# A 128-token unit of a gated recurrence: scores relative to the end of its first 64-token chunk, so that one pair of operands serves scores, output and state update

## The chip, the cores and the metric

The kernel runs on one core of a Trainium2 chip (trn2). The metric is the device time of one execution in microseconds; the kernel before took 1212.33 us, the median of three runs (1212.31 to 1212.84).

## What is computed

One inference step of a layer with three gated branches: 1024 prompt tokens and 32 sample tokens of width 1024 are normalised, multiplied with one combined weight matrix of 8192 columns, sent through branches A, B and C, merged and projected. The change lies in branch A alone, a gated linear recurrence with 4 heads of 128 columns, in chunks of 64 tokens:

```python
def step(s, inp):
    qc, lc, kc, vc = inp
    b = jnp.cumsum(lc, axis=2)
    qg = qc * jnp.exp(b)
    kg = kc * jnp.exp(-b)
    att = jnp.where(mask, jnp.einsum('bhtk,bhsk->bhts', qg, kg), 0.0)
    o = jnp.einsum('bhts,bhsv->bhtv', att, vc) + jnp.einsum('bhtk,bhkv->bhtv', qg, s)
    b_last = b[:, :, -1:, :]
    s = jnp.exp(b_last[:, :, 0, :])[..., None] * s + jnp.einsum('bhsk,bhsv->bhkv', kc * jnp.exp(b_last - b), vc)
    return s, o
```

Here `b` is the running sum of the log gates within a chunk, `qg` and `kg` are the query and key with the decay put in, and `s` is the state (128x128 per head). Afterwards each head's output is normalised, gated and projected down. The final states of prompt and sample are outputs too.

## The kernel before

Tokens stand in three groups of 384, 384 and 288 columns (the last holds 256 prompt and 32 sample tokens). All dense products are three-term: an operand is split into a high and a low part in a reduced float format, and each product is issued as high by high, high by low, low by high, so that one slot (`slot`) of 8 blocks is 24 matmuls at line 60 (`issue`). Weights come in tiles of 128 columns; `wprep` splits the next tile on ScalarE (`whi`, line 40) and VectorE (`wlo`, line 43) while the present one is used.

The order on each engine is that of the program (a manual schedule). The side work is written as generators that each slot advances: those in the list `fast` one step in the middle of a slot of 24 matmuls and one at its end, those in `slow` one step per slot. So a step of branch A's recurrence stands between stretches of 12 dense matmuls.

Branch A works head by head (`branch_a(j)`). Its four weight tiles give the forget gate, value, query and output gate (`psfa`, `psva`, `psqa`, `psga`). `chain` (in `slow`) makes the log gates, their running sum `b` by a scan that restarts every 64 tokens, `eb = exp(b)`, `kg = exp(-b)` times the key (lines 742, 743, 761) and `kd`, the key with the decay to its chunk's end (lines 746, 755, 762). `ev_va` and `tr_va` bring the values out of PSUM and transpose them on TensorE (lines 698, 706).

`hgrn` (in `fast`) then walks over 9 units: 8 of 128 prompt tokens, which are two chunks each, and one of 32 sample tokens. Its stages are staggered: step `t` issues `u0(t)`, `u2(t-1)`, `u4(t-2)`, `u3(t-1)`, `u1(t)`.

- `prep(g)` (lines 788 to 793, GpSimd) makes a second pair of operands for a group: `kd2`, the keys decayed to the end of the whole unit, and `qg2`, the queries with the decay from the unit's start.
- `u0` on TensorE: the scores within the chunks (line 807, `kg` by `qg`, 128x128), the scores of the second chunk's queries with the first chunk's keys (line 810, 64 columns of `kd` by 64 of `qg`, into 64x64), and a transpose of `kd2` (line 812).
- `u1`: VectorE puts the masked scores into `attm` (line 817) and the 64x64 block beside them (line 819); ScalarE copies the transposed keys out as `kt` (line 821).
- `u2` on TensorE: the state's increment (line 828, `kt` by `v`), the output from the scores (line 829), and the output from the old state `S` (line 831, with `qg2`).
- `u3`: VectorE makes the new state (line 842, old state times decay plus increment), ScalarE the square sum `sq` for the norm (line 849), GpSimd its inverse root (lines 155, 156).
- `u4` and `fin`: the scaled output `on` (line 856), three transposes back (line 863) and the gate (line 865).

The sample unit has no line 810. So a head issues line 810 eight times.

Of the kernel before, what the change touches and what calls it, by code (L numbers as in the profile page):

```python
# [7 lines left out]
F32 = mybir.dt.float32  # L8
# [3 lines left out]
OP = mybir.AluOpType  # L12
# [15 lines left out]
def kernel(ctx: ExitStack, tc: tile.TileContext, I, O):  # L28
# [647 lines left out]
    nc.gpsimd.memset(bd[0:64, 64:128], 0.0)  # L676
# [9 lines left out]
    def branch_a(j):  # L686
        R = {}
        f, lf, b, eb, kg, kd, va, qg, sg, el = {}, {}, {}, {}, {}, {}, {}, {}, {}, {}
        vs = ap.tile([32, 128], F32, tag="vs", name="vs")
        S0 = ap.tile([128, 128], F32, tag="S0", bufs=1, name="S0")  # L690

        def c64(t, g):
            nf = 6 if g < 2 else 4
            return t[:, :nf * 64].rearrange("p (c t) -> p c t", t=64), nf
# [29 lines left out]
        def chain():  # L724
            nc.sync.dma_start(S0, I["state_hgrn"][0, 0, j])
            for g in range(3):
                f[g] = T(g, "f")
                nc.scalar.activation(f[g], R["psfa", g], AF.Sigmoid)
                nc.vector.tensor_scalar(f[g], f[g], oml[:, j:j + 1], lb[:, j:j + 1], op0=OP.mult, op1=OP.add)
                if g < 2:  # L730
                    yield
# [8 lines left out]
            for g in range(3):  # L740
                eb[g], kg[g] = T(g, "eb"), T(g, "kg")
                nc.scalar.activation(eb[g], b[g], AF.Exp)
                nc.scalar.activation(kg[g], b[g], AF.Exp, scale=-1.0)
                bv, nf = c64(b[g], g)
                lv, _ = c64(lf[g], g)
                nc.vector.tensor_tensor(lv, bv[:, :, 63:64].to_broadcast([128, nf, 64]), bv, op=OP.subtract)
                if g == 2:
                    nc.vector.tensor_scalar(lf[g][:, 256:288], b[g][:, 256:288], -1.0, b[g][:, 287:288],
                                            op0=OP.mult, op1=OP.add)
# [3 lines left out]
            for g in range(3):  # L753
                kd[g] = lf[g]
                nc.scalar.activation(kd[g], lf[g], AF.Exp)
                ev, nf = c64(eb[g], g)
                el[g] = small.tile([128, 8], F32, tag="el", bufs=6, name="el")
                nc.gpsimd.tensor_copy(el[g][:, :nf], ev[:, :, 63])
                if g == 2:
                    nc.gpsimd.tensor_copy(el[g][:, 4:5], eb[g][:, 287:288])  # L760
                nc.vector.tensor_tensor(kg[g], kg[g], f[g], op=OP.mult)
                nc.gpsimd.tensor_tensor(kd[g], kd[g], f[g], op=OP.mult)
# [15 lines left out]
        def hgrn():  # L778
            qg2, kd2, elp, on = {}, {}, {}, {}

            def prep(g):
                npair = 3 if g < 2 else 2
                w = npair * 128
                qg2[g], kd2[g] = T(g, "qg2"), T(g, "kd2")
                v4 = lambda t: t[:, :w].rearrange("p (c h t) -> p c h t", h=2, t=64)
                eh = el[g][:, :2 * npair].rearrange("p (c h) -> p c h", h=2)
                bc = lambda h: eh[:, :, h:h + 1].to_broadcast([128, npair, 64])
                nc.gpsimd.tensor_scalar(v4(kd2[g])[:, :, 1, :], v4(kd[g])[:, :, 1, :], 1.0, 0.0, op0=OP.mult, op1=OP.add)
                nc.gpsimd.tensor_tensor(v4(kd2[g])[:, :, 0, :], v4(kd[g])[:, :, 0, :], bc(1), op=OP.mult)
                nc.gpsimd.tensor_scalar(v4(qg2[g])[:, :, 0, :], v4(qg[g])[:, :, 0, :], 1.0, 0.0, op0=OP.mult, op1=OP.add)  # L790
                nc.gpsimd.tensor_tensor(v4(qg2[g])[:, :, 1, :], v4(qg[g])[:, :, 1, :], bc(0), op=OP.mult)
                elp[g] = small.tile([128, 4], F32, tag="elp", name="elp")
                nc.gpsimd.tensor_tensor(elp[g][:, :npair], eh[:, :, 0], eh[:, :, 1], op=OP.mult)

            units = [(g, c) for g in range(3) for c in range(3)]
            nu = len(units)
            pu, po, at, kt, rs, Ss = {}, {}, {}, {}, {}, {-1: None}
# [6 lines left out]
            def u0(u):  # L804
# [3 lines left out]
                if not smp:  # L808
                    c0 = c * 128
                    nc.tensor.matmul(p[0:64, 128:192], kd[g][:, c0:c0 + 64], qg[g][:, c0 + 64:c0 + 128],  # L810
                                     start=True, stop=True)
                nc.tensor.transpose(p[:m, 192:320], kd[g][:, sl] if smp else kd2[g][:, sl], ident)  # L812

            def u1(u):
# [3 lines left out]
                if not smp:  # L818
                    nc.vector.tensor_copy(a[0:64, 64:128], pu[u][0:64, 128:192])
                kt[u] = ap.tile([128, 128], F32, tag="kt", name="kt")  # L820
                nc.scalar.activation(kt[u][:m], pu[u][:m, 192:320], AF.Copy)

            def u2(u):
                g, c, smp, m, sl = geo(u)
                vv = vs if smp else va[g][:, sl]
                S = S0 if smp else Ss[u - 1]
                po[u] = abank("po")
                nc.tensor.matmul(pu[u][:, 320:448], kt[u][:m], vv, start=True, stop=True)
                nc.tensor.matmul(po[u][:m, 0:128], at[u][:m, :m], vv, start=True, stop=(S is None))
                if S is not None:  # L830
                    nc.tensor.matmul(po[u][:m, 0:128], qg[g][:, sl] if smp else qg2[g][:, sl], S,
                                     start=False, stop=True)

            def u3(u):
                g, c, smp, m, sl = geo(u)
                S = S0 if smp else Ss[u - 1]
                Sn = Ss[u] = ap.tile([128, 128], F32, tag="S", bufs=3, name="S")
# [303 lines left out]
```

## Time and profile before

| | |
|---|---|
| runs | 1212.31, 1212.33, 1212.84 us |
| profiled execution, first to last instruction (its span) | 1210.8 us |
| TensorE (PE) busy | 1193.9 us, 99% |
| PE's weight loads (PEld), which overlap it | 1170.2 us, 97% |
| VectorE (DVE) busy | 548.6 us, 45% |
| ScalarE (ACT) busy | 477.0 us, 39% |
| GpSimd (POOL) busy | 267.5 us, 22% |
| mean granted TensorE clock | 0.998 of full |

For the profiled execution the span is the time that is shown; the runs' median is 1.5 us longer. Busy time of PE is a model: matmuls are pipelined, each lasts longer than the distance to the next one's start, and so the price of a matmul is read as the distance between two starts in the timeline, not as its duration. A plain fp32 matmul is one line of the program and two on PE (x2 in the timeline); a transpose and a split product are one.

### The profile page before, as it was taken

The page shows a single profiled execution, that of the slowest core. Times are in us where ns is not written, and L with a number is a line of the kernel's source. Part 1 is how long each engine was busy: PE and PEld are TensorE (multiplying, and loading weights), DVE is VectorE, ACT ScalarE, POOL GpSimd, SP SyncE. Part 2 cuts the span into 40 slices and gives each one's busy share as a digit, 9 for nine tenths or more (in the row PEclk, how much of TensorE's full clock was granted, in tenths as well). Part 3 has the DMA queues.
Part 4 walks back from the last instruction along what each step waited for, and adds up shares of the span by engine and source line. Part 5 has one row for each costly group of instructions (what it writes and reads, how often), then busy time and mean ns, then how long its engine had stood idle before and what let it go on. Part 6 is the DMA issues. An engine that isn't in the chain of part 4 may idle for free.

```text
span 1210.8 us, 18948 instructions
## 1 busy us (share of the span) xinstructions
PE 1193.9 (99%) x7630; PEld 1170.2 (97%) x7630; DVE 548.6 (45%) x1088; ACT 477.0 (39%) x1015; POOL 267.5 (22%) x478
## 2 busy tenths in 40 slices
PE   7999999999999999999999999999999999999998
PEld 7899999999999999999999999999999999999996
DVE  4957775257611234454545421223465541337322
ACT  6567667366711114252525221111344452224211
POOL 3413222022201242333323201223000001224101
PEclk9999999999999999999999999999999999999999
DMA  8521101211111121010111111102111112105321
GB/s 263 172 64 38 40 21 44 79 37 38 44 42 39 44 62 53 19 51 27 45 33 43 35 48 35 53 27 75 44 45 38 29 45 70 54 27 174 105 92 40
DMA packets 113564, 70.65 MB, mean 58 GB/s; under 512 B 5560, under 2 KB 109668, under 8 KB 113476
## 3 DMA queue, kind: packets, MB, share of 16 engines
q1 hardware_dynamic: 113476, 69.44, 19.1%
q8 instruction: 60, 0.98, 0.3%
q14 instruction: 28, 0.23, 0.1%
HBM read 63.49 MB, written 5.93 MB: 57 GB/s over the span
## 4 chain that ended last, share of the span: by engine, by line
PE 94%; DVE 2%; DMA 2%; ACT 1%; issue 1%; SPq 0%; POOL 0%; POOLq 0%; DVEq 0%; ACTq 0%
PE psz L60 23%; PE psdn L60 15%; PE psout L60 8%; PE psgb L60 8%; PE psxb L60 7%; PE psfa L60 4%; PE psva L60 4%; PE psga L60 4%; PE psqc L60 4%; PE psqa L60 4%; PE psgc L60 3%; PE pr L60 1%; PE pi L60 1%; PE poc L60 1%; PE pu L812 1%; PE pssa L60 1%
## 5 line engine op out<-in xcount | busy, mean ns | idle before, releaser
L43 DVE TENSOR_TENSOR wlo<-wraw,whi 128x1024 fp32r<-128x1024 f32 (+1 forms) x100 | 107.9, 1079 | 263.1 <-ACT whi L40 261.9
L60 PE MATMUL psz<-hh,whi 128*128 128x384 f32 (+1 forms) x576 | 185.9, 323 | 0.0
L60 PE MATMUL psz<-hh,wlo 128*128 128x384 f32 (+1 forms) x576 | 185.1, 321 | 0.0
L60 PE MATMUL psz<-hl,whi 128*128 128x384 f32 (+1 forms) x576 | 185.0, 321 | 0.0
L40 ACT ACTIVATE whi<-wraw 128x1024 fp32r<-128x1024 f32 (+1 forms) x104 | 96.3, 926 | 82.9 <-PE psdn L60 74.1
L60 PE MATMUL psdn<-pl,whi 128*128 128x384 f32 (+1 forms) x384 | 124.2, 323 | 0.0
L60 PE MATMUL psdn<-ph,whi 128*128 128x384 f32 (+1 forms) x384 | 124.1, 323 | 0.0
L60 PE MATMUL psdn<-ph,wlo 128*128 128x384 f32 (+1 forms) x384 | 124.1, 323 | 0.0
L60 PEld LDWEIGHTS psz<-hh,whi 128*128 128x128 f32 x576 | 108.1, 188 | 0.7 <-issue 0.6
L60 PEld LDWEIGHTS psz<-hh,wlo 128*128 128x128 f32 x576 | 108.2, 188 | 0.3 <-DVE wlo L43 0.3
L60 PEld LDWEIGHTS psz<-hl,whi 128*128 128x128 f32 x576 | 108.1, 188 | 0.0
L584 ACT ACTIVATE sz<-psz 128x384 f32<-128x384 f32 (+1 forms) x72 | 33.3, 463 | 181.8 <-PE psz L60 181.7
L60 PEld LDWEIGHTS psdn<-ph,whi 128*128 128x128 f32 x384 | 72.1, 188 | 0.0
L60 PEld LDWEIGHTS psdn<-pl,whi 128*128 128x128 f32 x384 | 72.1, 188 | 0.0
L60 PEld LDWEIGHTS psdn<-ph,wlo 128*128 128x128 f32 x384 | 72.1, 188 | 0.0
L60 PE MATMUL psout<-hh,mhi 128*128 128x384 f32 (+3 forms) x216 | 68.8, 319 | 0.0
L60 PE MATMUL psout<-hh,mlo 128*128 128x384 f32 (+3 forms) x216 | 68.8, 319 | 0.0
L60 PE MATMUL psout<-hl,mhi 128*128 128x384 f32 (+3 forms) x216 | 68.8, 318 | 0.0
L60 PE MATMUL psxb<-hh,wlo 128*128 128x384 f32 (+1 forms) x192 | 62.1, 324 | 0.0
L60 PE MATMUL psxb<-hh,whi 128*128 128x384 f32 (+1 forms) x192 | 61.9, 323 | 0.0
L60 PE MATMUL psxb<-hl,whi 128*128 128x384 f32 (+1 forms) x192 | 61.8, 322 | 0.0
L60 PE MATMUL psgb<-hh,whi 128*128 128x384 f32 (+1 forms) x192 | 61.8, 322 | 0.0
(308 smaller groups left out, 2957.9 us busy)
## 6 DMA issues: line engine op xcount, KB each, us to landing
wraw<-in_w_in SPq DMA_DIRECT2D x64, 512.0 KB, 4.1
xt<-in_x_prompt SPq DMA_DIRECT2D x8, 512.0 KB, 5.2
wraw<-in_w_b_down SPq DMA_DIRECT2D x16, 256.0 KB, 2.8
wraw<-in_w_out SPq DMA_DIRECT2D x8, 512.0 KB, 3.8
xf<-in_x_prompt SPq DMA_DIRECT2D x8, 512.0 KB
out<-yf SPq DMA_DIRECT2D x8, 512.0 KB, 2.9
wraw<-in_w_mem_k SPq DMA_DIRECT2D x4, 512.0 KB, 4.1
wraw<-in_w_mem_v SPq DMA_DIRECT2D x4, 512.0 KB
```

The costliest lines, as they stand in the source:

```text
L40: nc.scalar.activation(out, in_, AF.Copy)
L43: (eng or nc.vector).tensor_tensor(out, a, hi.bitcast(F32), op=OP.subtract)
L60: nc.tensor.matmul(ps, a, b, start=st, stop=sp)
L584: nc.scalar.activation(s, R["psz", g], AF.Sigmoid)
L812: nc.tensor.transpose(p[:m, 192:320], kd[g][:, sl] if smp else kd2[g][:, sl], ident)
```

## The change

Within a unit the running sums are shifted so that both chunks count from the end of the first chunk. For the first chunk VectorE subtracts the sum at its last token (`dm`, taken out by small GpSimd copies) from `b` before the two exponentials. Then `kg` and `qg` give all scores of the unit in one 128x128 product under a plain triangular mask, the transposed `kg` serves the state update, and `qg` serves the output from the state. What is carried from unit to unit is now `R`, the state relative to that point (VectorE); ScalarE makes `Sn` from it with one factor per row, `dec`, which stands in `qg`'s frame and is what the next unit's matmul reads. `prep`, `kd`, `kd2`, `qg2`, `el`, `elp`, line 810's matmul and line 819's copy go.

```diff
--- before.py
+++ after.py
@@ -667,13 +667,12 @@
     down(lambda k: prods_b[4 + k], C_ZB, "second", AH_B)
     ap = next_phase("ap", 2)
     bd = ap.tile([128, 128], F32, bufs=1, name="bd")
     nc.gpsimd.memset(bd, 1.0)
     nc.gpsimd.affine_select(bd, bd, pattern=[[1, 128]], compare_op=OP.is_ge, fill=0.0,
                             base=0, channel_multiplier=-1)
-    nc.gpsimd.memset(bd[0:64, 64:128], 0.0)
     attm = [ap.tile([128, 128], F32, bufs=1, name=f"attm{i}") for i in range(2)]
     for t in attm:
         nc.gpsimd.memset(t, 0.0)
@@ -685,13 +684,11 @@
     def branch_a(j):
         R = {}
-        f, lf, b, eb, kg, kd, va, qg, sg, el = {}, {}, {}, {}, {}, {}, {}, {}, {}, {}
+        f, lf, b, eb, kg, va, qg, sg = {}, {}, {}, {}, {}, {}, {}, {}
         vs = ap.tile([32, 128], F32, tag="vs", name="vs")
         S0 = ap.tile([128, 128], F32, tag="S0", bufs=1, name="S0")
-
-        def c64(t, g):
-            nf = 6 if g < 2 else 4
-            return t[:, :nf * 64].rearrange("p (c t) -> p c t", t=64), nf
+        dm = ap.tile([128, 20], F32, tag="dm", name="dm")
+        dec = ap.tile([128, 9], F32, tag="dec", name="dec")
         def ev_va(g):
             vT = T(g, "vT")
@@ -723,6 +720,7 @@
         def chain():
             nc.sync.dma_start(S0, I["state_hgrn"][0, 0, j])
+            nc.gpsimd.memset(dm[:, 8:10], 0.0)
             for g in range(3):
                 f[g] = T(g, "f")
                 nc.scalar.activation(f[g], R["psfa", g], AF.Sigmoid)
@@ -738,28 +736,26 @@
             ev_va(0)
             yield
             for g in range(3):
+                npair = 3 if g < 2 else 2
                 eb[g], kg[g] = T(g, "eb"), T(g, "kg")
+                bv = b[g][:, :npair * 128].rearrange("p (c h t) -> p c h t", h=2, t=64)
+                u = 3 * g
+                nc.gpsimd.tensor_copy(dm[:, u:u + npair], bv[:, :, 0, 63])
+                nc.gpsimd.tensor_copy(dm[:, 10 + u:10 + u + npair], bv[:, :, 1, 63])
+                nc.vector.tensor_tensor(bv[:, :, 0, :], bv[:, :, 0, :],
+                                        dm[:, u:u + npair].unsqueeze(2).to_broadcast([128, npair, 64]),
+                                        op=OP.subtract)
+                if g == 2:
+                    nc.gpsimd.tensor_copy(dm[:, 18:19], b[g][:, 287:288])
                 nc.scalar.activation(eb[g], b[g], AF.Exp)
                 nc.scalar.activation(kg[g], b[g], AF.Exp, scale=-1.0)
-                bv, nf = c64(b[g], g)
-                lv, _ = c64(lf[g], g)
-                nc.vector.tensor_tensor(lv, bv[:, :, 63:64].to_broadcast([128, nf, 64]), bv, op=OP.subtract)
-                if g == 2:
-                    nc.vector.tensor_scalar(lf[g][:, 256:288], b[g][:, 256:288], -1.0, b[g][:, 287:288],
-                                            op0=OP.mult, op1=OP.add)
+            nc.gpsimd.tensor_tensor(dec, dm[:, 10:19], dm[:, 1:10], op=OP.add)
+            nc.scalar.activation(dec, dec, AF.Exp)
             tr_va(0)
             ev_va(1)
             yield
             for g in range(3):
-                kd[g] = lf[g]
-                nc.scalar.activation(kd[g], lf[g], AF.Exp)
-                ev, nf = c64(eb[g], g)
-                el[g] = small.tile([128, 8], F32, tag="el", bufs=6, name="el")
-                nc.gpsimd.tensor_copy(el[g][:, :nf], ev[:, :, 63])
-                if g == 2:
-                    nc.gpsimd.tensor_copy(el[g][:, 4:5], eb[g][:, 287:288])
                 nc.vector.tensor_tensor(kg[g], kg[g], f[g], op=OP.mult)
-                nc.gpsimd.tensor_tensor(kd[g], kd[g], f[g], op=OP.mult)
             tr_va(1)
             ev_va(2)
             yield
@@ -776,25 +772,10 @@
                 yield
         def hgrn():
-            qg2, kd2, elp, on = {}, {}, {}, {}
-
-            def prep(g):
-                npair = 3 if g < 2 else 2
-                w = npair * 128
-                qg2[g], kd2[g] = T(g, "qg2"), T(g, "kd2")
-                v4 = lambda t: t[:, :w].rearrange("p (c h t) -> p c h t", h=2, t=64)
-                eh = el[g][:, :2 * npair].rearrange("p (c h) -> p c h", h=2)
-                bc = lambda h: eh[:, :, h:h + 1].to_broadcast([128, npair, 64])
-                nc.gpsimd.tensor_scalar(v4(kd2[g])[:, :, 1, :], v4(kd[g])[:, :, 1, :], 1.0, 0.0, op0=OP.mult, op1=OP.add)
-                nc.gpsimd.tensor_tensor(v4(kd2[g])[:, :, 0, :], v4(kd[g])[:, :, 0, :], bc(1), op=OP.mult)
-                nc.gpsimd.tensor_scalar(v4(qg2[g])[:, :, 0, :], v4(qg[g])[:, :, 0, :], 1.0, 0.0, op0=OP.mult, op1=OP.add)
-                nc.gpsimd.tensor_tensor(v4(qg2[g])[:, :, 1, :], v4(qg[g])[:, :, 1, :], bc(0), op=OP.mult)
-                elp[g] = small.tile([128, 4], F32, tag="elp", name="elp")
-                nc.gpsimd.tensor_tensor(elp[g][:, :npair], eh[:, :, 0], eh[:, :, 1], op=OP.mult)
-
+            on = {}
             units = [(g, c) for g in range(3) for c in range(3)]
             nu = len(units)
-            pu, po, at, kt, rs, Ss = {}, {}, {}, {}, {}, {-1: None}
+            pu, po, at, kt, rs, Rs, Ss = {}, {}, {}, {}, {}, {}, {0: None, 8: S0}
             def geo(u):
                 g, c = units[u]
@@ -805,44 +786,42 @@
                 g, c, smp, m, sl = geo(u)
                 p = pu[u] = abank("pu")
                 nc.tensor.matmul(p[:m, 0:m], kg[g][:, sl], qg[g][:, sl], start=True, stop=True)
-                if not smp:
-                    c0 = c * 128
-                    nc.tensor.matmul(p[0:64, 128:192], kd[g][:, c0:c0 + 64], qg[g][:, c0 + 64:c0 + 128],
-                                     start=True, stop=True)
-                nc.tensor.transpose(p[:m, 192:320], kd[g][:, sl] if smp else kd2[g][:, sl], ident)
+                nc.tensor.transpose(p[:m, 128:256], kg[g][:, sl], ident)
             def u1(u):
                 g, c, smp, m, sl = geo(u)
                 a = at[u] = attm[u % 2]
                 nc.vector.copy_predicated(a[:m, :m], bd[:m, :m].bitcast(U32), pu[u][:m, 0:m])
-                if not smp:
-                    nc.vector.tensor_copy(a[0:64, 64:128], pu[u][0:64, 128:192])
                 kt[u] = ap.tile([128, 128], F32, tag="kt", name="kt")
-                nc.scalar.activation(kt[u][:m], pu[u][:m, 192:320], AF.Copy)
+                nc.scalar.activation(kt[u][:m], pu[u][:m, 128:256], AF.Copy)
             def u2(u):
                 g, c, smp, m, sl = geo(u)
                 vv = vs if smp else va[g][:, sl]
-                S = S0 if smp else Ss[u - 1]
+                S = Ss[u]
                 po[u] = abank("po")
-                nc.tensor.matmul(pu[u][:, 320:448], kt[u][:m], vv, start=True, stop=True)
+                nc.tensor.matmul(pu[u][:, 256:384], kt[u][:m], vv, start=True, stop=True)
                 nc.tensor.matmul(po[u][:m, 0:128], at[u][:m, :m], vv, start=True, stop=(S is None))
                 if S is not None:
-                    nc.tensor.matmul(po[u][:m, 0:128], qg[g][:, sl] if smp else qg2[g][:, sl], S,
-                                     start=False, stop=True)
+                    nc.tensor.matmul(po[u][:m, 0:128], qg[g][:, sl], S, start=False, stop=True)
             def u3(u):
                 g, c, smp, m, sl = geo(u)
-                S = S0 if smp else Ss[u - 1]
-                Sn = Ss[u] = ap.tile([128, 128], F32, tag="S", bufs=3, name="S")
-                if S is None:
-                    nc.vector.tensor_copy(Sn, pu[u][:, 320:448])
+                R = Rs[u] = ap.tile([128, 128], F32, tag="R", bufs=2, name="R")
+                if u == 0:
+                    nc.vector.tensor_copy(R, pu[u][:, 256:384])
+                elif smp:
+                    nc.vector.tensor_tensor(R, pu[u][:, 256:384], S0, op=OP.add)
                 else:
-                    dec = el[g][:, 4:5] if smp else elp[g][:, c:c + 1]
-                    nc.vector.scalar_tensor_tensor(Sn, S, dec, pu[u][:, 320:448], op0=OP.mult, op1=OP.add)
-                if smp:
+                    nc.vector.scalar_tensor_tensor(R, Rs[u - 1], dec[:, u - 1:u], pu[u][:, 256:384],
+                                                   op0=OP.mult, op1=OP.add)
+                Sn = ap.tile([128, 128], F32, tag="S", bufs=3, name="S")
+                nc.scalar.activation(Sn, R, AF.Copy, scale=dec[:, u:u + 1])
+                if u < 7:
+                    Ss[u + 1] = Sn
+                elif smp:
                     nc.sync.dma_start(O[7][0, 0, j], Sn)
-                elif u == 7:
+                else:
                     nc.sync.dma_start(O[2][0, 0, j], Sn)
                 sq = ap.tile([128, 128], F32, tag="sq", bufs=1, name="sq")
                 ss = small.tile([128, 1], F32, tag="ss", name="ss")
@@ -866,7 +845,6 @@
                 prods_a[j][g] = prod_split(s, g)
             prods_a[j] = {}
-            prep(0)
             yield
             yield
             for t in range(nu + 4):
@@ -880,8 +858,6 @@
                     u3(t - 1)
                 if t < nu:
                     u1(t)
-                if t in (1, 3):
-                    prep((t + 1) // 2)
                 if t >= 5 and (t - 5) % 3 == 0:
                     fin((t - 5) // 3)
                 yield
```

On TensorE, step 3 of a head (`u0` of unit 3, `u2` of unit 2; `pu` holds scores, transposed keys and increment of a unit, `po` its output, `psga` the dense product around it; `lf` is the buffer of `kd`):

```order
 L60 MATMUL psga<-hh_84,wlo 128x384
-L807 MATMUL pu<-q,kg 128x128
-L810 MATMUL pu<-q,lf 64x64
-L812 MATMUL pu<-ident,kd_5222 128x128
-L828 MATMUL pu<-v,kt 128x128
-L829 MATMUL po<-v,attm_4814 128x128
-L831 MATMUL po<-S,qg_5144 128x128
+L788 MATMUL pu<-q,kg 128x128
+L789 MATMUL pu<-ident,kg 128x128
+L803 MATMUL pu<-v,kt 128x128
+L804 MATMUL po<-v,attm_4813 128x128
+L806 MATMUL po<-S,q 128x128
```

The 64x64 matmul between the scores and the transpose is gone; the others stand in the same order, and the transpose reads the operand that the scores have just read.

On ScalarE, two later steps of the same head (`sga` is the output gate's evacuation), before:

```order
L721 ACTIVATE sga<-psga 128x384
L849 ACTIVATE sq,ss<-po 128x128
L821 ACTIVATE kt<-pu 128x128
L849 ACTIVATE sq,ss<-po 128x128
L821 ACTIVATE kt<-pu 128x128
```

and with the change:

```order
L718 ACTIVATE sga<-psga 128x384
L819 ACTIVATE S<-R,dec 128x128
L828 ACTIVATE sq,ss<-po 128x128
L796 ACTIVATE kt<-pu 128x128
L819 ACTIVATE S<-R,dec 128x128
L828 ACTIVATE sq,ss<-po 128x128
L796 ACTIVATE kt<-pu 128x128
```

Each step has one more instruction, the scaled copy of the state, ahead of the square sum and of `kt`.

On VectorE, step 2 of a head and the start of step 3, before:

```order
L856 TENSOR_SCALAR on<-po,rsr 128x128
L842 SCALAR_TENSOR_TENSOR S<-S,elp,pu 128x128
L817 COPY_PREDICATED attm_4814<-bd,pu 128x128
L819 COPY attm_4814<-pu 64x64
L856 TENSOR_SCALAR on<-po,rsr 128x128
```

and with the change:

```order
L835 TENSOR_SCALAR on<-po,rsr 128x128
L816 SCALAR_TENSOR_TENSOR R<-R,dec,pu 128x128
L794 COPY_PREDICATED attm_4813<-bd,pu 128x128
L835 TENSOR_SCALAR on<-po,rsr 128x128
```

The copy of the 64x64 block is gone, and the state's update writes `R` in the place of `S`.

## Rows read from the trace of the kernel before

**Rows 1.** The page: span, busy time of TensorE, and its granted clock in 40 slices.
```profile
span 1210.8 us, 18948 instructions
...
PE 1193.9 (99%) x7630; PEld 1170.2 (97%) x7630; DVE 548.6 (45%) x1088; ACT 477.0 (39%) x1015; POOL 267.5 (22%) x478
...
PEclk9999999999999999999999999999999999999999
```

**Rows 2.** Instructions in order of time, PE, one step: start us, us, engine, line, operands.
```profile
506.90 0.34 PE L60 MATMUL psfa<-hh,wlo 128*128 128x384 f32 x1
507.07 0.38 PE L807 MATMUL pu<-q,kg 128*128 128x128 f32 x2
507.38 0.33 PE L810 MATMUL pu<-q,lf 128*64 128x64 f32 x2
507.64 0.33 PE L812 MATMUL pu<-ident,kd 128*128 128x128 f32 x1
507.81 0.39 PE L828 MATMUL pu<-v,kt 128*128 128x128 f32 x2
508.03 0.39 PE L829 MATMUL po<-v,attm 128*128 128x128 f32 x2
508.26 0.39 PE L831 MATMUL po<-S,qg 128*128 128x128 f32 x2
508.40 0.42 PE L60 MATMUL psfa<-hh,whi 128*128 128x384 f32 x1
```

**Rows 3.** The same view and step, PE's weight loads.
```profile
507.38 0.19 PEld L810 LDWEIGHTS pu<-q,lf 128*64 128x64 f32 x2
507.64 0.14 PEld L812 LDWEIGHTS pu<-ident,kd 128*128 128x128 f32 x1
...
507.92 0.30 PEld L829 LDWEIGHTS po<-v,attm 128*128 128x128 f32 x2
```

**Rows 4.** The same view, PE, the sample unit's step and three transposes.
```profile
514.39 0.28 PE L812 MATMUL pu<-ident,lf 128*32 128x128 f32 x1
514.51 0.39 PE L828 MATMUL pu<-v,kt 128*128 128x128 f32 x2
...
514.95 0.39 PE L831 MATMUL po<-S,qg 128*128 128x128 f32 x2
515.18 0.49 PE L863 MATMUL pot<-ident,on 128*128 128x128 f32 x3
...
515.68 0.34 PE L60 MATMUL psfa<-hl,whi 128*128 128x384 f32 x1
```

**Rows 5.** Instructions on tile `pu`: duration ns min/median/max, first and last start, forms.
```profile
L810 PE MATMUL pu<-q,lf x64: 222/246/270, 487.9 to 694.6; 128*64 128x64 f32 x64
...
L812 PE MATMUL pu<-ident,kd x32: 328/328/330, 488.2 to 694.8; 128*128 128x128 f32 x32
```

**Rows 6.** In order of time, ACT, DVE and PE around the sample unit's `kt`.
```profile
512.77 1.05 ACT L40 ACTIVATE whi<-wraw 128x1024 fp32r<-128x1024 f32 x1
...
515.65 0.34 DVE L842 SCALAR_TENSOR_TENSOR S<-S,elp,pu 128x128 f32<-128x128 f32 x1
...
516.11 0.27 ACT L821 ACTIVATE kt<-pu 32x128 f32<-32x128 f32 x1 [0.29 <-DVE attm L817]
...
517.69 0.48 PE L828 MATMUL pu<-vs,kt 32*128 32x128 f32 x2
```

**Rows 7.** In order of time, POOL, DVE, ACT and PE in the stage of the exponentials.
```profile
464.01 2.65 POOL L737 TENSOR_SCALAR f<-f 128x384 f32<-128x384 f32 x3 [10.21 <-ACT lf L735]
...
468.51 1.35 DVE L746 TENSOR_TENSOR lf<-b 128x384 f32<-128x384 f32 x3
...
468.65 0.53 ACT L742 ACTIVATE eb<-b 128x384 f32<-128x384 f32 x1
...
470.99 0.47 ACT L698 ACTIVATE vT<-psva 128x384 f32<-128x384 f32 x1
...
473.32 0.49 PE L706 MATMUL ptv<-ident,vT 128*128 128x128 f32 x3
```

## The prediction, made before the changed kernel had run

> **What bounds the kernel now.** I read the page first, then PE's instructions in order of time, then the other engines in the same stretch. On the page PE is busy for 1193.9 us of a span of 1210.8 us, with the granted clock in its top tenth in every slice [rows 1]. No other engine is above 45%. So the kernel ends when PE has worked off its list, and a change is worth what it takes off PE's list, less what PE then has to wait for.
>
> The price of a matmul on PE is the distance from its start to the next start. In one step of branch A [rows 2] the dense product before it takes 0.17 us (506.90 to 507.07). Then line 807 takes 0.31 us, line 810 takes 0.26, line 812 takes 0.17, and lines 828 and 829 together 0.45 (507.81 to 508.26), so about 0.225 each. Lines 807, 828 and 829 are the same kind of work: a plain fp32 product with a 128x128 stationary operand and 128 columns. Line 807 costs 0.09 us more than the other two. The weight loads show why [rows 3]: line 829's load starts at 507.92, 0.11 us before its matmul, while its predecessor still runs. Line 810's load starts at 507.38, in the same instant as its matmul, and so does line 812's at 507.64. Around the 64-column matmul the loads are not hidden. It is not only its own 0.26 us that PE pays, but a bubble at both its edges.
>
> What a transpose costs without such a bubble is seen in [rows 4]: three transposes and one dense product take 515.18 to 515.68, 0.50 us; less 0.17 for the dense one, 0.33 for three, 0.11 each. The entry into them from line 831, a plain product, takes 0.23 us (514.95 to 515.18), as between plain products. And in the sample unit, which has no line 810, line 812 takes 0.12 us before a line 828 that carries the same wait for `kt` (514.39 to 514.51). So the 0.17 us of line 812 in the other units are 0.11 us and a bubble of 0.055.
>
> **The sum.** Line 810 is on PE 64 times [rows 5], two for each fp32 product: 32 products, 8 units by 4 heads; line 812 of that form is there 32 times too. Per unit:
>
> - before, from line 807 to line 828: 507.81 - 507.07 = 0.74 us [rows 2];
> - with the change, scores and transpose alone: 0.225 (as lines 828 and 829) + 0.11 (as line 863) = 0.335 us.
>
> That is 0.405 us less per unit, and 32 x 0.405 = 13.0 us. The first unit of each head is followed by a dense product instead of line 828; I give it the same price. The sample units keep their two matmuls, and lines 828, 829, 831 and 863 keep theirs.
>
> The Trainium skill bears on this in TensorEngine Tiling (Array Packing), section Key Properties: changing the tiling mode, and not only the tile, drains the engine. Read for a change in the number of stationary columns, it agrees with the weight loads of lines 810 and 812 [rows 3], and the two drains go with line 810, so the sum stays 13.0 us. Read for any change of mode, a transpose's own mode among them, it would leave a drain where line 789 follows line 788; that is rival B below, and the entry from line 831 into line 863 at 0.23 us [rows 4] speaks against it.
>
> **What lies beside it, at nothing.** PE covers all of this as long as it isn't made to wait.
>
> - *GpSimd* loses `prep` and gets small copies; it was 22% busy. *VectorE* loses 32 copies (line 819) and half the width of line 746. *ScalarE* loses 12 exponentials (line 755) and gets 36 scaled copies and 4 small exponentials. None of them is near PE's 99%.
> - *The scaled copy on ScalarE.* It stands ahead of `sq` and `kt`, and waits for VectorE's `R`. Behind it are queued `kt`, for which the next step's line 803 waits, and the norm's `sq`. The tightest place before is the sample unit's `kt` [rows 6]: it ends at 516.38, and line 828 starts at 517.69, 1.31 us later. There VectorE's update ran late, 515.65 to 515.99. With the change the copy starts at about 516.0 and lasts, as `kt`, 0.27 us; `sq` and its accumulator read follow, and `kt` ends at some 516.8, 0.4 us later than before. If the step is also 0.405 us shorter, 0.5 us are left. Elsewhere `kt` has more. `Sn` itself is wanted later still, behind lines 803 and 804.
> - *The exponentials' stage.* `eb` now waits for VectorE's subtraction, and that for two GpSimd copies. GpSimd is free at 464.01 + 2.65 = 466.66, and VectorE came to the subtraction (line 746 before) at 468.51 [rows 7], so 1.85 us are there for two tiny copies; the three 384- and 288-column operations before them took 0.88 each, a bound from above. `eb` started at 468.65; a subtraction at line 746's full width, 1.35 / 3 = 0.45 us, moves it to 469.0 at most. Add `dec`'s exponential, at most `eb`'s 0.53 us, and `vT` of the second group ends at 470.99 + 0.47 + 0.35 + 0.53 = 472.3 at the latest. PE's transpose of it starts at 473.32. It still isn't waited for.
>
> So nothing on the other side of the sum. The profiled span would go from 1210.8 to 1197.8 us; the runs' median is 1.5 us above the span, and 1212.3 - 13.0 = **1199.3 us**.
>
> **Bounds of what the trace doesn't show.** That line 789 follows line 788 directly, with the same stationary operand, has no row. Between 0.335 and 0.48 us for the pair are the ends: 0.31 + 0.17 if line 788 keeps line 807's price and the transpose line 812's, all read in [rows 2]. I take 0.335, because line 831 into line 863 and the sample unit's line 812 [rows 4] are the nearest rows. The ends give 13.0 and 32 x 0.26 = 8.3 us.
>
> **The rivals.**
>
> - *A: the transpose keeps 0.17 us* because the instruction behind it waits for a semaphore on `kt`, and only line 788 gets cheaper. Pair 0.225 + 0.17, gain 32 x 0.345 = 11.0 us: **1201.3 us**. For it: every line 812 at 0.17 us has a waiting line 828 behind it. Against: the sample unit's has one too and takes 0.12 us.
> - *B: only line 810's own place goes*, since the entry into a transpose drains in the way the entry into line 810 does. Gain 8.3 us: **1204.0 us**. Against: 0.23 us from line 831 to line 863. The Trainium skill's sentence on drains (TensorEngine Tiling, Key Properties), read widely, would give this.
> - *C: slower than before.* ScalarE becomes the bound of the recurrence: the scaled copy waits for `R`, and `kt` behind it comes too late for line 803. It decides from the point at which `kt` is over 0.9 us later than before (1.31 less the 0.405 by which the step shrinks). My sum has 0.4. If a weight split, 1.05 us [rows 6], stood in every step ahead of `kt` as well, `kt` would be 1.45 us late, PE would wait 0.55 us per unit, 32 x 0.55 = 17.6 us against a gain of 13.0: **1216.9 us**. Against: a weight tile is 6 steps long, so a split falls into one or two steps of a head.
> - *D: the same with two such steps in each head*: 8 x 0.55 = 4.4 us lost, 13.0 - 4.4 = 8.6 us gained: **1203.7 us**.
> - *E: the change is not worth anything*, since PE waits for something else in the freed time. PE has next to no idle time in the trace, so there is no such wait to fall back on: about 1212 us.
>
> **How the numbers follow.** A measurement of this kernel tells about 0.2% (2.4 us) from no change. Forecast 0.62, A 0.17, B 0.09, D 0.07, E 0.03, C 0.02. Faster by over 0.2% are the forecast, A, B and D: 0.95; same is E, 0.03; slower is C, 0.02. The range takes in the forecast, A, B and D, whose times are also the bounds of the pair's price: from 1198.3 (the forecast less 1 us for rounding of the rows, 32 x 0.01, and the runs' spread of 0.5) to 1204.3 us.
>
> **What would show it.** In the changed profile line 788 to line 789 should be 0.22 us, line 789 to line 803 0.11 us, and line 789's weight load should start before line 788 ends. PE's busy share stays at 99%, with no wait of PE for `kt` or `S`. A distance of 0.31 and 0.17 would mean B, 0.22 and 0.17 A; a wait of line 803 for line 796 would mean C or D. The forecast is wrong if the span shrinks by under 12 or over 14 us.

## The result, and the profile after

The changed kernel takes 1196.45 us, the median of 4 runs (1195.67 to 1198.16), against 1212.32 for the kernel before: a ratio of 0.9874, 95% interval 0.9861 to 0.9887. Run again against 21 runs of the kernel before, it took 1196.96 us, ratio 0.9874 (0.9861 to 0.9888). That is 15.3 us less (13.6 to 16.9). The forecast was 1199.3 us, 13.0 less, in a range of 1198.3 to 1204.3. The direction was right; the gain was larger than the forecast, and the time lies below the range.

The page of the changed kernel, which answers to [rows 1]:

```profile
span 1194.4 us, 18697 instructions
...
PE 1179.8 (99%) x7566; PEld 1161.6 (97%) x7566; DVE 539.1 (45%) x1052; ACT 479.9 (40%) x1043; POOL 236.0 (20%) x425
...
PEclk9999999999999999999999999999999999999999
```

PE is as full as before, and its list is 64 lines shorter, the 32 products of line 810. One step of the recurrence in the changed kernel, PE and then its weight loads, in order of time (start us, us, engine, line, operands); it answers to [rows 2, 3]:

```profile
501.87 0.38 PE L788 MATMUL pu<-q,kg 128*128 128x128 f32 x2
502.09 0.27 PE L789 MATMUL pu<-ident,kg 128*128 128x128 f32 x1
502.20 0.39 PE L803 MATMUL pu<-v,kt 128*128 128x128 f32 x2
502.42 0.39 PE L804 MATMUL po<-v,attm 128*128 128x128 f32 x2
```
```profile
501.70 0.36 PEld L788 LDWEIGHTS pu<-q,kg 128*128 128x128 f32 x2
501.98 0.14 PEld L789 LDWEIGHTS pu<-ident,kg 128*128 128x128 f32 x1
```

Scores 0.22 us, transpose 0.11 us, together 0.33 where the kernel before had 0.74; and the transpose's weights load from 501.98, 0.11 us before its matmul. This is the pair as it was forecast.

Where the time went is read from four places that both programs have: the first product of branch B (`psxb`), the first of branch A (`psfa`), branch A's last group of transposes (`pot`), and the last product of all (`psout`). In order of time, PE, the kernel before:

```profile
51.88 0.42 PE L60 MATMUL psxb<-hh,whi 128*128 128x384 f32 x1
...
449.94 0.33 PE L60 MATMUL psfa<-hh,whi 128*128 128x384 f32 x1
...
705.65 0.56 PE L863 MATMUL pot<-ident,on 128*128 128x128 f32 x3
...
1204.86 0.28 PE L60 MATMUL psout<-hh,mlo 128*32 128x256 f32 x1
```

The changed kernel:

```profile
49.87 0.43 PE L60 MATMUL psxb<-hh,whi 128*128 128x384 f32 x1
...
447.21 0.34 PE L60 MATMUL psfa<-hh,whi 128*128 128x384 f32 x1
...
689.69 0.55 PE L842 MATMUL pot<-ident,on 128*128 128x128 f32 x3
...
1188.41 0.28 PE L60 MATMUL psout<-hh,mlo 128*32 128x256 f32 x1
```

Branch A, from `psfa` to `pot`, went from 255.71 to 242.48 us: 13.23 less. The forecast for it was 13.0. But 2.01 us are gone ahead of `psxb`, 0.72 between `psxb` and `psfa`, and 0.49 behind `pot`: 3.2 us, in places where the two programs have the same instructions on PE. These are what the experiments are about, beside the reasons for the 13.2.

### The profile page after: what moved, and what is told of

Same layout as the page of the kernel before. It is cut to its first block, busy times and chain, and to the rows that moved or that the text cites. A ratio compares the mean times of both kernels' runs of the same rounds, so it can differ in the third digit from the quotient of the medians.

```text
span 1194.4 us, 18697 instructions
## 1 busy us (share of the span) xinstructions
PE 1179.8 (99%) x7566; PEld 1161.6 (97%) x7566; DVE 539.1 (45%) x1052; ACT 479.9 (40%) x1043; POOL 236.0 (20%) x425
## 4 chain that ended last, share of the span: by engine, by line
PE 92%; DVE 4%; DMA 2%; issue 1%; ACT 1%; SPq 0%; POOL 0%; POOLq 0%; DVEq 0%; ACTq 0%
PE psz L60 23%; PE psdn L60 14%; PE psgb L60 8%; PE psxb L60 7%; PE psout L60 7%; PE psfa L60 4%; PE psva L60 4%; PE psga L60 4%; PE psqa L60 4%; PE psqc L60 4%; PE psgc L60 3%; PE pr L60 1%; PE pi L60 1%; PE poc L60 1%; DVE ht L241 1%; PE pssa L60 1%
## 5 line engine op out<-in xcount | busy, mean ns | idle before, releaser
L60 PE MATMUL psgb<-hh,wlo 128*128 128x384 f32 (+1 forms) x192 | 61.7, 321 | 0.0
```

Source lines behind the costliest of these rows:

```text
L60: nc.tensor.matmul(ps, a, b, start=st, stop=sp)
```

## The experiments

### Both kernels again

No edit. The first question was whether the 3.2 us outside branch A come back.

> The kernel before once more, unchanged. Question: of the 16.4 us between the two profiled spans 13.3 lie inside branch A and 2.1 in the first 35 us, where the two programs are the same. Theory 1 (scatter of the start): in this run the first dense product of branch B (psxb) starts somewhere between 49.5 and 52 us, not always at 51.9, and the median stays at 1211 to 1213 us. Theory 2 (the changed program starts faster in itself, by another layout in memory): psxb starts at 51.9 us again within 0.3 us, and ratio 1.000.

> The changed kernel once more, unchanged. Both theories: branch A from its first psfa to the last pot matmul is 13.3 us shorter than in the kernel before. Theory 1 (scatter): psxb starts anywhere from 49.5 to 52 us, and the gain over five rounds settles at 13.3 to 14.5 us (ratio 0.988 to 0.989). Theory 2 (systematic start): psxb starts at 49.9 us again, the gain stays at 15.5 to 16 us (ratio 0.987).

The kernel before took 1212.17 us (ratio 1.0003, 0.9994 to 1.0011), the changed one 1196.96, ratio 0.9874: a gain of 15.1 us by medians, more than the 13.3 to 14.5 of the first theory and less than the 15.5 to 16 of the second. The changed kernel's places, second execution:

```profile
52.52 0.42 PE L60 MATMUL psxb<-hh,whi 128*128 128x384 f32 x1
...
449.82 0.34 PE L60 MATMUL psfa<-hh,whi 128*128 128x384 f32 x1
...
692.30 0.55 PE L842 MATMUL pot<-ident,on 128*128 128x128 f32 x3
...
1190.43 0.28 PE L60 MATMUL psout<-hh,mlo 128*32 128x256 f32 x1
```

`psxb` starts at 52.52 here and at 49.87 in the first execution of the same program; in the kernel before it was 51.88 and then 50.17. So the 2 us at the start are scatter; in this the first theory is right. The rest is not: `psxb` to `psfa` is 397.30 us (397.34 in the first execution, 398.06 in the kernel before), branch A 242.48 again, and `pot` to `psout` 498.13 (498.72, and 499.21 before). Some 1.2 to 1.8 us outside branch A are systematic, and for these neither the prediction nor the two theories had a mechanism.

The start in numbers, busy time by engine, in two stretches of 20 us (behind the last busy time the granted clock, DMA share, GB/s), the changed kernel and then its second execution:

```profile
0.00:20.00 20.00, 15.91 (x103) 15.49 (x104) 9.24 (x10) 11.30 (x17) 4.93 (x16) 0.91 0.80 266
20.00:40.00 20.00, 19.20 (x163) 18.62 (x160) 16.92 (x22) 15.19 (x28) 13.00 (x13) 1.00 0.85 268
```
```profile
0.00:20.00 20.00, 15.44 (x92) 15.21 (x93) 7.84 (x9) 9.94 (x15) 3.13 (x14) 0.83 0.78 264
20.00:40.00 20.00, 17.96 (x150) 17.20 (x150) 15.82 (x18) 14.70 (x26) 12.06 (x12) 1.00 0.74 235
```

In both PE has gaps in the first 20 us and part of that stretch runs at the lower clock level (1.2 GHz; mean granted clock 0.91 and 0.83), and the second execution moved less data in the next stretch, 235 against 268 GB/s. What sets one or the other was not tried.

### The 64-column matmul put back, and taken out alone

`a_64` puts a matmul of line 810's shape back into the changed kernel; `b_no64` takes line 810 (and line 819's copy) out of the kernel before. The latter leaves out the scores of a unit's second chunk with its first, so branch A's output is not the layer's; its time alone is of use. The edit of `a_64`:

```diff
                 nc.tensor.matmul(p[:m, 0:m], kg[g][:, sl], qg[g][:, sl], start=True, stop=True)
+                if not smp:
+                    c0 = c * 128
+                    nc.tensor.matmul(p[0:64, 384:448], kg[g][:, c0:c0 + 64], qg[g][:, c0 + 64:c0 + 128],
+                                     start=True, stop=True)
```

and of `b_no64`:

```diff
-                if not smp:
-                    c0 = c * 128
-                    nc.tensor.matmul(p[0:64, 128:192], kd[g][:, c0:c0 + 64], qg[g][:, c0 + 64:c0 + 128],
-                                     start=True, stop=True)
...
-                if not smp:
-                    nc.vector.tensor_copy(a[0:64, 64:128], pu[u][0:64, 128:192])
```

> The changed kernel with a matmul of 64 stationary by 64 moving columns put back between scores and transpose, in each of the 32 prompt units; nobody reads its result. Theory 1 (the gain is the matmul and the two drains at its edges): lines 788 to 789 become 0.31 + 0.26 and the transpose 0.165 us again, 0.405 us more per unit, 13.0 us more than the changed kernel, so 1209 to 1210 us. Rival (part of the gain came from the relief of GpSimd, VectorE and ScalarE): clearly under 13 us more, at most 8.3.

> The kernel before without line 810's matmul and line 819's copy: the scores of a unit's second chunk with its first are left out, all else of the old scheme (prep on GpSimd, kd, kd2, qg2) stays. Theory 1: the whole gain in branch A, 13.0 to 13.3 us, is here too, 1198 to 1199.5 us; line 807 to line 812 0.22, line 812 to line 828 0.11 us. Rival (operands from one pair are needed for the cheap pair, since line 789 loads what line 788 has just loaded): 0.31 and 0.17 us, a gain of 8.3 us, 1204 us.

`a_64` took 1209.84 us (ratio to the kernel before 0.998, 0.9972 to 0.9989), 12.9 more than the changed kernel. In order of time, PE, one step:

```profile
505.76 0.38 PE L788 MATMUL pu<-q,kg 128*128 128x128 f32 x2
506.07 0.33 PE L791 MATMUL pu<-q,kg 128*64 128x64 f32 x2
506.33 0.33 PE L793 MATMUL pu<-ident,kg 128*128 128x128 f32 x1
506.50 0.39 PE L807 MATMUL pu<-v,kt 128*128 128x128 f32 x2
```

The scores cost 0.31 us again, the narrow product 0.26, the transpose 0.17: 0.74, as in [rows 2], with the new scheme around them. The weight loads of the narrow product and of the transpose start at 506.07 and 506.33, in the same instants as their matmuls, as in [rows 3]. `b_no64` took 1198.81 us (ratio 0.9888, 0.9873 to 0.9903), a gain of 13.2 by medians. In its step:

```profile
503.07 0.38 PE L807 MATMUL pu<-q,kg 128*128 128x128 f32 x2
503.29 0.27 PE L808 MATMUL pu<-ident,kd 128*128 128x128 f32 x1
503.40 0.39 PE L822 MATMUL pu<-v,kt 128*128 128x128 f32 x2
```

0.22 and 0.11 us, though scores and transpose load different operands. So branch A's gain is line 810's place and its two edges; the single pair of operands, and the work taken off GpSimd and VectorE, give PE nothing that these runs can tell. Both rivals fall. And `a_64`, which has all of the change but this, is still 2.2 us below the kernel before: the systematic rest again.

### A full product in the narrow one's place

```diff
+                if not smp:
+                    nc.tensor.matmul(p[:m, 384:512], kg[g][:, sl], qg[g][:, sl], start=True, stop=True)
```

> The changed kernel with a full plain product (128 stationary columns, 128 moving) between scores and transpose, whose result nobody reads. Theory (line 810 paid for two drains at its edges): 0.22 us per unit without drains, 32 x 0.22 = 7.0 us more than the changed kernel, so less than the 64-column one that is half its size and cost 13. Rival (any third product in this place costs this much): 13 us more.

1205.24 us (ratio 0.9945, 0.9931 to 0.9959), 8.3 more than the changed kernel by medians, where 7.0 was expected and the rival had 13; in the profile branch A is 7.3 us longer. One step, PE:

```profile
504.13 0.38 PE L788 MATMUL pu<-q,kg 128*128 128x128 f32 x2
504.35 0.39 PE L790 MATMUL pu<-q,kg 128*128 128x128 f32 x2
504.58 0.27 PE L791 MATMUL pu<-ident,kg 128*128 128x128 f32 x1
504.69 0.39 PE L805 MATMUL pu<-v,kt 128*128 128x128 f32 x2
```

0.22, 0.23, 0.11: the product with twice the stationary and twice the moving columns costs 0.23 us where the narrow one cost 0.41 with its edges; 32 x 0.23 = 7.4 us. Its weight load starts at 504.24, 0.11 us before its matmul. The Trainium skill's rule that a change of tiling mode drains the engine (TensorEngine Tiling (Array Packing), Key Properties) agrees in its narrow reading: a change of stationary columns from 128 to 64 and back raises the product ahead to 0.31 us and the transpose behind to 0.17, the entry into a transpose alone does not (0.22 and 0.11). That the engine drains there is the Trainium skill's word; the traces show the price and the late weight loads. This pair of runs changes stationary and moving columns together; products with a narrow stationary operand and 128 moving columns come in the last experiment.

### Where the tiles lie

The change also drops two small tiles, `el` and `elp`. By the programs' allocations, every tile behind them lies 384 bytes per partition lower. The down projections (`psdn`) read their moving operands there, in four phases of 288 products, all outside branch A; their stationary operands and results lie at the same addresses in all these programs. `a_pad` allocates the two tiles again, unused; `b_shift` puts 128 bytes into the kernel before, `a_off128` and `a_off256` 128 and 256 bytes into the changed one. The edit of `a_pad`:

```diff
+    for tag in ("el", "elp"):
+        nc.gpsimd.memset(small.tile([128, 4], F32, tag=tag, bufs=6, name=tag), 0.0)
```

and of `b_shift` and `a_off128` (`a_off256` has `bufs=8`):

```diff
+    nc.gpsimd.memset(small.tile([128, 4], F32, tag="pad", bufs=4, name="pad"), 0.0)
```

> The changed kernel with the two small tiles it dropped (el, elp: 6 buffers of 32 bytes each per partition) allocated again and not used, so that all tiles behind them lie 384 bytes higher, where the kernel before has them. The down projections of branches A, B and C (psdn) have the same instructions in both kernels, but cost 0.176 us per 384-column product before and 0.1735 with the change. Theory (address): the rate of psdn depends on where the tiles lie; here it is 0.176 us again, the stretches outside branch A are as before, and the run takes 1.2 to 1.6 us more than the changed kernel. Rival (something else in the change, such as the shorter program): psdn stays at 0.1735 and the time at the changed kernel's.

> The kernel before with 128 bytes per partition of unused tiles put in, so that the tiles behind lie at the same place within 512 bytes as in the changed kernel (384 lower there, 128 higher here). Theory, first form (the place within 256 or 512 bytes counts): psdn 0.1735 us, 1.2 to 1.6 us faster than before, 1210.6 us. Theory, second form (another place counts), and rival (not addresses): psdn 0.176 us, time as before.

> The changed kernel with the tiles behind the small ones 128 bytes higher. The operands of psdn then start at 96 within every 256 bytes, as in the kernel before, where it was slow; but at 96 within 512, where the kernel before had 352. If the place within 256 bytes decides: psdn 0.176 us per 384-column product. If only the place 352 within 512 is bad: 0.1735.

> The changed kernel with the tiles behind the small ones 256 bytes higher: 224 within 256 bytes, as in the changed kernel, and 224 within 512, where the changed kernel has 480. If the place within 256 bytes decides: psdn 0.1735 us. If the place within 512 decides, it may be either.

The first phase is read from its first product to the `psxb` behind its last, PE in order of time; the third line is the first product of the second phase. The kernel before, and the changed kernel:

```profile
186.43 0.34 PE L60 MATMUL psdn<-ph,whi 128*128 128x384 f32 x1
...
232.94 0.33 PE L60 MATMUL psxb<-hh,whi 128*128 128x384 f32 x1
...
357.47 0.34 PE L60 MATMUL psdn<-ph,whi 128*128 128x384 f32 x1
```
```profile
184.35 0.33 PE L60 MATMUL psdn<-ph,whi 128*128 128x384 f32 x1
...
230.40 0.34 PE L60 MATMUL psxb<-hh,whi 128*128 128x384 f32 x1
...
354.93 0.34 PE L60 MATMUL psdn<-ph,whi 128*128 128x384 f32 x1
```

The changed kernel with 128 bytes put in, and with 256:

```profile
183.99 0.34 PE L60 MATMUL psdn<-ph,whi 128*128 128x384 f32 x1
...
230.51 0.33 PE L60 MATMUL psxb<-hh,whi 128*128 128x384 f32 x1
```
```profile
183.81 0.33 PE L60 MATMUL psdn<-ph,whi 128*128 128x384 f32 x1
...
229.85 0.34 PE L60 MATMUL psxb<-hh,whi 128*128 128x384 f32 x1
```

46.51 and 46.05 us, then 46.52 and 46.04: two values and nothing between. All profiles fall into these two:

| kernel | where the moving operands of the 384-column products start, within 256 bytes | first phase of `psdn`, us |
|---|---|---|
| before, `b_again`, `b_no64`, `a_pad`, `a_off128` | 96 | 46.5 |
| after, `a_again`, `a_64`, `a_128`, `b_shift`, `a_off256`, `a_wide`, `a_act8`, `a_act3b` | 224 | 46.0 |

The place within 256 bytes decides, of the places tried; within 512 it does not, since 352 and 96 are slow and 480 and 224 fast. In each of the four phases the mean distance from a 384-column product to the next is 0.1758 to 0.1761 us in the upper row and 0.1735 to 0.1741 in the lower; of the 288-column products a part lies at the other place in every kernel.

The whole phases do not all gain as much as the first. The second, from the third lines above to the first `psfa`, went from 92.5 to 92.3 us; each read from its first product to the one behind its last, the four gained 0.48, 0.21, 0.44 and 0.38 us, 1.5 us in all. `b_shift`, the kernel before with 128 unused bytes, gains 1.4 us in them, and took 1210.41 us (ratio 0.9984, 0.9975 to 0.9993), 1.9 us faster than before. `a_pad` loses 1.8 us in them against the changed kernel, and took 1199.63 us (ratio 0.9898, 0.9884 to 0.9912), 2.7 more; that is more than the 1.2 to 1.6 expected. The single runs of `a_off128` and `a_off256` took 1197.78 and 1195.45 us. Why one place is slower was not found; all tiles behind the small ones move together, so the operands' own place and that of what other engines use meanwhile are not told apart.

`a_pad` also tells the instructions from the addresses: it has the changed kernel's instructions, with the place of the dropped tiles kept. Its branch A:

```profile
448.51 0.33 PE L60 MATMUL psfa<-hh,whi 128*128 128x384 f32 x1
...
691.17 0.56 PE L844 MATMUL pot<-ident,on 128*128 128x128 f32 x3
```

It takes 242.66 us, 13.05 less than the 255.71 of the kernel before, so some 0.2 of the 13.23 come with the addresses too. And its 1199.63 us, 12.6 below the kernel before by medians (10.7 to 14.1), are close to what the instructions alone give.

### The cover of `kt`

Copies on ScalarE, ahead of `kt` in every step, in the changed kernel: 8 (`a_act8`), then 3 (`a_act3b`; `a_act3`, the same with a slip in another line, gave no result).

```diff
+                kx = ap.tile([128, 128], F32, tag="kx", bufs=1, name="kx")
+                for _ in range(8):
+                    nc.scalar.activation(kx[:m], pu[u][:m, 128:256], AF.Copy)
                 nc.scalar.activation(kt[u][:m], pu[u][:m, 128:256], AF.Copy)
```

> The changed kernel with 8 copies of 128x128 from PSUM put on ScalarE ahead of kt in every step, 0.17 us each by their spacing, so kt comes 1.36 us later. In the changed profile kt ends 0.45 us before line 803 in unit 2, 0.8 in units 3 and 8, 0.96 in unit 4, 1.3 in unit 1. Theory (kt's cover is that slack): PE waits about 0.9, 0.55, 0.6, 0.4 and 0.05 us in these, 2.5 per head, 8 to 12 us in all over the changed kernel. Rival (the cover is larger or smaller than these distances): under 4 or over 16 us.

> The experiment with the extra copies on ScalarE again, with 3 copies. The 8 copies took 0.31 us each (they write one buffer), not 0.17, and the time rose by 69 us. Theory (cover of kt is the distance read in the changed profile: 0.45 us in unit 2, 0.8 in units 3 and 8, 0.96 in unit 4): kt comes 0.93 us later, PE waits 0.5, 0.13, 0.15 us, 0.8 per head, 3 us in all; 2 to 5 us over the changed kernel. Rival (any lateness of kt feeds on itself from step to step, as the 69 us may say): over 10 us.

8 copies: 1266.06 us (ratio 1.0448, 1.0433 to 1.0462), 69 more than the changed kernel. The theory's 8 to 12 us fail, and the rival's bound of over 16 is passed by far. The copies took 2.43 us and not 1.36; they all write one buffer, which may be why, but no run with several buffers tells. PE waits 49.2 us for `kt` in the profile, and the granted clock stands at its lower level (1.2 GHz) for 23.9 us of branch A, where the changed kernel's profile has none; so the 69 us are not a price of lateness alone.

```profile
490.93 2.43 ACT L798 ACTIVATE kx<-pu 128x128 f32<-128x128 f32 x8
493.25 0.27 ACT L799 ACTIVATE kt<-pu 128x128 f32<-128x128 f32 x1
```

3 copies: 1207.05 us (ratio 0.9951, 0.9932 to 0.9971), 10.1 more; the theory had 2 to 5, and its rival, that lateness feeds on itself from step to step, over 10. In its profile they put `kt` 0.78 us later (the first starts at 490.13, `kt` at 490.91), not 0.93. PE's waits in this kernel (us in total, times, longest), and three of them in the first head, with the wait in brackets:

```profile
PE pu L806 <- ACT kt L799: 7.7, 12, 1.0
```
```profile
495.97 0.49 PE L806 MATMUL pu<-v,kt 128*128 128x128 f32 x2 [1.00 <-ACT kt L799]
...
501.68 0.49 PE L806 MATMUL pu<-v,kt 128*128 128x128 f32 x2 [0.25 <-ACT kt L799]
...
515.48 0.48 PE L806 MATMUL pu<-vs,kt 32*128 32x128 f32 x2 [0.76 <-ACT kt L799]
```

The waits fall in three units of each head: units 2, 4 and 8. In unit 2 the wait is 1.00 us where 0.93 - 0.45 = 0.5 was expected. There `kt` starts 2.76 us later than in the changed kernel, and PE without the wait would be 1.36 later: a lateness of 1.4 us, nearly twice 0.78. That unit comes behind a step in which ScalarE also splits weights: `whi` is late by the copies, VectorE's `wlo` waits for `whi`, `R` stands behind `wlo`, and the scaled copy with three more copies behind `R`. So the lateness of two steps adds up there (read from the order in the trace, not tried). The remaining 2.4 us of the 10.1 fall beside the waits that the profile names. So rivals C and D name a mechanism that this kernel has: 0.78 us more per step on ScalarE cost 10 us, and the theory that only the cover of each step counts was wrong.

### No narrow operand in the sample unit either

The sample unit's 32 tokens are put into a unit of 128, the rest set to zero (core of the edit):

```diff
-        vs = ap.tile([32, 128], F32, tag="vs", name="vs")
+        vs = ap.tile([128, 128], F32, tag="vs", name="vs")
...
+            nc.gpsimd.memset(vs, 0.0)
...
+                    nc.gpsimd.memset(kg[g][:, 288:384], 0.0)
...
-                return g, c, smp, (32 if smp else 128), slice(c * 128, c * 128 + (32 if smp else 128))
+                return g, c, smp, 128, slice(c * 128, c * 128 + 128)
```

> The changed kernel with the sample unit made 128 tokens wide (96 columns of kg and qg and 96 rows of v set to zero), so that none of its matmuls has 32 stationary columns or 32 rows. Theory (PE pays for drains where a narrow stationary operand stands between wide ones): from the last psfa ahead of its three output matmuls to the second one behind them 0.98 us instead of 1.59, the scores' stretch 0.06 shorter, the last three transposes 0.1 to 0.25 shorter: 0.8 to 0.95 us per head, 3.2 to 3.8 us in all, 1193 us. Rival (narrow operands are as cheap as wide ones and only their number counts): no gain, or a small loss.

1193.18 us (ratio 0.984, 0.9826 to 0.9853): 3.8 us less than the changed kernel, the fastest of all here, and a version that beats both. From the last `psfa` ahead of the sample's three products to the second behind them, the changed kernel and then this one:

```profile
511.39 0.34 PE L60 MATMUL psfa<-hh,wlo 128*128 128x384 f32 x1
511.66 0.48 PE L803 MATMUL pu<-vs,kt 32*128 32x128 f32 x2
...
512.98 0.30 PE L60 MATMUL psfa<-hl,whi 128*128 128x288 f32 x1
```
```profile
511.77 0.34 PE L60 MATMUL psfa<-hh,wlo 128*128 128x384 f32 x1
511.95 0.38 PE L809 MATMUL pu<-vs,kt 128*128 128x128 f32 x2
...
512.75 0.29 PE L60 MATMUL psfa<-hl,whi 128*128 128x288 f32 x1
```

1.59 and 0.98 us, as expected, with 128 tokens in the place of 32. All three products have 128 moving columns in both kernels, so it is not the number of moving columns that makes the difference here. In the changed kernel their weight loads, and that of the dense product behind them, start in the same instants as the matmuls (511.66, 512.07, 512.40, 512.74); in this one each starts 0.11 us or more before its matmul, but for the dense product's (0.03).

## Why the prediction was wrong

By its own steps:

- *PE bounds the kernel, and the price is the distance between starts.* Right: 99% before and after, and no wait for `kt` or `S` in the changed profile.
- *The sum of branch A, 13.0 us.* Right: 13.23, of which 13.05 remain at the old addresses (`a_pad`). Scores and transpose at 0.22 and 0.11 us are the forecast's prices, rivals A (0.17 for the transpose) and B (0.31 and 0.17) are refuted by the changed profile itself, and `b_no64`, `a_64` and `a_128` show that line 810 and its two edges are all of it.
- *What lies beside it, at nothing.* This step failed, in a place it did not look at. It counted instructions added and removed, and asked who waits. It did not ask what the dropped tiles do to the addresses of those behind them. `el` and `elp` moved the down projections' operands by 384 bytes, from 96 to 224 within 256, and the four phases of `psdn` became 1.5 us shorter; the stretches outside branch A and the start, 1.2 to 1.8 us. 13.2 + 1.5 makes some 14.7 of the 15.3 us; the rest lies within the interval. With the tiles left where they were, `a_pad` took 1199.63 us, against the forecast's 1199.3.
- *The cover of `kt`.* Right in the result, with a wrong place: the tightest was not the sample unit (0.77 us left in the changed profile, forecast 0.5) but unit 2, with 0.45 us, where the kernel before had 1.38. "Elsewhere `kt` has more" was read from the kernel before; with the change unit 2 lost 0.93 us of it.
- *The range.* Its lower end allowed 1 us below the forecast, for rounding and a spread of 0.5 us read from three runs. The same program's start alone differs by 2.65 us between two executions (49.87 and 52.52), and 21 runs of the kernel before lay between 1210.59 and 1213.72. No case in the text had more gain than the sum, so nothing held the range open on that side.
- *The span to shrink by 12 to 14 us*, the text's own test: it shrank by 16.4, of which 2.0 were the scatter of the start.

## What to carry to other kernels

Where PE is full, look for matmuls whose stationary operand has fewer columns or rows than their neighbours': they cost their own place and an unhidden weight load at either edge, more than a full-width product, and padding with zeros can be cheaper. Price them from the distance between starts and from whether the weight load starts before its matmul. When a change drops or adds a tile, check where the tiles behind it come to lie (a run that allocates the dropped tile unused tells the two effects apart), and leave room in the range for stretches that the change doesn't touch.

## What the runs showed that was not expected

- The same 288 products of `psdn` take 46.5 or 46.0 us with the place of their moving operands, 96 or 224 within 256 bytes; fourteen profiles of twelve programs fall into the one or the other without exception.
- A product with 128 stationary and 128 moving columns costs 0.23 us between products of its kind, one with 64 and 64 costs 0.41 us with its edges.
- The first 50 us of the same program differ by up to 2.65 us between executions, with different stretches at the lower clock.
